# Start bytes of the standing weights: 108 and 364 instead of 224 and 512

## The chip, the cores and the metric

The kernel runs on one core of a Trainium2 chip. The metric is the device time of one launch in microseconds. Three runs of the kernel before gave 2774.83, 2776.44 and 2776.48 us, a median of 2776.44 us. Beside them stands one profiled execution of the same program, from which every row in this document is taken.

## The reference

The reference is a trunk of two decoder layers on 256 tokens of width 2048 in float32. Layer 0 mixes tokens by gated DeltaNet (16 key heads, 32 value heads of 128), layer 1 by HGRN2 (16 heads of 128); each mixer is followed by a SwiGLU feed-forward of width 5632. Cut to what matters here:

```python
h = x
for layer in range(2):
    n = rmsnorm(h, mixer_norm[layer])
    h = h + (gdn_mixer, hgrn2_mixer)[layer](n, ...)   # n @ w_in, recurrence in chunks, @ w_out
    h = h + swiglu(rmsnorm(h, ffn_norm[layer]), w_gate[layer], w_up[layer], w_down[layer])
return rmsnorm(h, final_norm)
```

Nearly all of the arithmetic is in the large products n @ w with weights that are read from HBM once. The products are wanted at close to float32 accuracy.

## The kernel before, in words

**How a large product is computed.** All weights come as halves of tiles, 128 partitions by 1024 float32 (512 KB). The function `stream` (line 587) walks through all halves of all groups in one list. For each half a DMA on SyncE's queue lands it in `raw`; ScalarE copies it to `wh`, rounded to the type float32r; VectorE writes what is left, raw - wh, to `wl`, again float32r. The activations are split in the same manner into `xt_h` and `xt_l` (in other stages `hth` and `htl`, `ot_h` and `ot_l`). A product is then three float32r products that add up in PSUM: high by high, high by low, low by high. There are four buffers each of raw, wh and wl, and loads run three halves ahead.

**Two ways to multiply.** `mm_rows` (line 624) lets the activations stand (128 by 128 tokens) and moves 512 weight columns per product; this covers the values and gates of the mixers, their output projections and the feed-forwards. `mm_cols` (line 652) lets 128 weight columns stand and moves all 256 tokens, so that the result comes out transposed, with features on the partitions. It serves the keys and queries of gated DeltaNet (8 groups) and the forget gates and queries of HGRN2 (8 groups). In one half it makes two 128-row blocks by four 128-column blocks by three products:

```python
for f in range(n_f):
    at = (k * n_f + f) * P
    for m, (w, s) in enumerate(((wh, xh), (wh, xl), (wl, xh))):
        self.nc.tensor.matmul(ps[...], w[:, at : at + P], s, ...)
```

Names in the profile read out<-moving,standing, so these products are main<-xt_h,wh, main<-xt_l,wh and main<-xt_h,wl. Each has a weight load of its own (PEld, LDWEIGHTS), also where two in a row use the same weights. Groups made with `cols=True` (lines 1292 and 1596) are the ones that use `mm_cols`. `mm_gates` (line 667) also lets weights stand, 64 columns wide, 48 products in all; its group is made without `cols=True`.

**Where wh and wl lie.** A partition of such a tile holds 1024 float32 (4096 bytes), and each tile is made 64 float32 (256 bytes, `PAD`) longer. The eight of them, alternately wh and wl, lie one behind the other and begin at byte 32 and byte 288 modulo 512 in turn. `make` (line 446) then chooses how many float32 to skip at the front so that the data begins at a wanted byte modulo 512, and `actual` (line 460) adds that skip to every access, of ScalarE, VectorE and TensorE alike:

```python
n = v.pool.padded.setdefault((v.tag, v.slot), len(v.pool.padded))
at = 32 + n * v.pad * 4 % 512
want = IN_COLS[v.tag] if v.cols else 32 + n % 2 * 512
v.skip = (want - at) // 4
```

For groups with `cols=True` the wanted bytes are those of `IN_COLS` (line 77); for all others both tiles begin at 32 modulo 512 (544 is 32 modulo 512). The same buffer can serve both kinds in turn, with another skip each time. A block of 128 columns is 512 bytes, so every block that stands begins at the same byte modulo 512 as its tile; in the gates a block is 256 bytes, so that blocks begin at 32 and 288 in turn. The token tiles xt_h and xt_l, whose slices are 1024 bytes, lie at byte 32 modulo 512 throughout, as follows from the sizes of the tiles allocated ahead of them; so do the tiles w and dec of the DeltaNet stage.

**What sets the order.** The whole program is recorded first; a planner (`plan`, line 308) then places every instruction on its engine by a list of costs (`price`, line 260) and due times, and the order that comes out is issued as written. The costs are computed from shapes and kinds of instruction. The large products form one fixed sequence on TensorE; the small products of the recurrences (aux in the profile) are put between them.

Of the kernel before, what the change touches and what calls it, by code (L numbers as in the profile page):

```python
# [73 lines left out]


PAD = 64
IN_COLS = {"wh": 224, "wl": 512}


class Op:  # L80
# [68 lines left out]
class Recorder:  # L149
# [296 lines left out]
    def make(self, v):  # L446
# [3 lines left out]
        if v.pad:  # L450
# [4 lines that stand above are left out]
# [1306 lines left out]
```

## Time and profile before

| what | value |
|---|---|
| median of three runs | 2776.44 us |
| span of the profiled execution | 2773.0 us |
| TensorE busy | 2757.2 us, 99% |
| weight loads under way | 2340.8 us, 84% |
| VectorE busy | 1901.0 us, 69% |
| ScalarE busy | 1428.3 us, 52% |
| products with 128 weight columns standing | 3 x 1024 |
| products with 512 weight columns moving, in main | 3 x 2176, 3 x 664 and 3 x 384 |

The profile's own record of the execution is the span, from the first to the last instruction; it stands 3.4 us under the median of the runs. All instructions carry line 490, where the recorded program is issued, so groups are told apart by the names of their tiles and by their shapes. A group's row gives busy time and the mean length of one record, then the idle time of the engine ahead of it and who ended it. Records of products overlap on TensorE, so a mean length isn't the pace; the pace is read from starts in the timeline or from a piece of the chain with its count. Products with standing weights fill TensorE from 8.9 us on in stretches up to 1898 us, between stretches with moving weights.

### The profile page before, as it was taken

The numbers are of one execution on the slowest core, as the hardware profiler recorded it, in microseconds if no ns is written. First come the engines' busy times: TensorE is split into PE (matmuls) and PEld (weight loads), VectorE is DVE, ScalarE is ACT, GpSimd is POOL, SyncE is SP. The second block draws the span as 40 slices with busy tenths as digits, with TensorE's granted clock in tenths as the row PEclk, the third lists the DMA queues.
The fourth block names the chain that finished last, engine by engine and source line by source line (L and its number), as shares of the span: only waits on it lengthen the run. The fifth ranks groups of instructions, "written<-read, shape, count | busy, mean of one in ns | idle before, by whom it ended". The sixth has DMA issues, their size and how long they took to land.

```text
span 2773.0 us, 41091 instructions
## 1 busy us (share of the span) xinstructions
PE 2757.2 (99%) x15662; PEld 2340.8 (84%) x15662; DVE 1901.0 (69%) x2857; ACT 1428.3 (52%) x2010; POOL 251.2 (9%) x370
## 2 busy tenths in 40 slices
PE   9999999999999999999999999999999999999998
PEld 9888888888888888888888989988888888888887
DVE  6787888878766666546665687778656675456764
ACT  6656666565554444344444556556454444344443
POOL 1213222232110000000000100000110000000000
PEclk9999999999999999999999999999999999999999
DMA  7686568786676555666556645545675556665564
GB/s 256 196 280 223 183 214 278 213 276 217 223 255 208 192 195 192 225 222 195 192 194 218 217 164 175 169 166 175 226 265 192 196 192 210 222 208 194 193 201 160
DMA packets 162677, 580.52 MB, mean 209 GB/s; under 512 B 20138, under 2 KB 21306, under 8 KB 162352
## 3 DMA queue, kind: packets, MB, share of 16 engines
q1 hardware_dynamic: 138912, 503.15, 55.4%
q0 software_dynamic: 23280, 73.91, 8.4%
q8 instruction: 122, 2.00, 0.3%
q10 hardware_dynamic: 288, 0.85, 0.1%
q14 instruction: 75, 0.61, 0.1%
HBM read 550.52 MB, written 27.31 MB: 208 GB/s over the span
## 4 chain that ended last, share of the span: by engine, by line
PE 99%; ACT 0%; DVE 0%; issue 0%; POOLq 0%; POOL 0%; ACTq 0%
PE main L490 92%; PE aux L490 6%; ACT dec L490 0%; DVE wl L490 0%; ACT wh L490 0%; ACT xt_h L490 0%; DVE utmp L490 0%; DVE u L490 0%; DVE pre L490 0%; ACT y L490 0%; POOLq L1757 0%; ACT junk L490 0%; DVE xl L490 0%; POOL coll L490 0%; DVE xt_l L490 0%
## 5 line engine op out<-in xcount | busy, mean ns | idle before, releaser
L490 DVE TENSOR_TENSOR wl<-raw,wh 128x1024 fp32r<-128x1024 f32 x945 | 1160.6, 1229 | 759.8 <-ACT wh L490 749.1
L490 ACT ACTIVATE wh<-raw 128x1024 fp32r<-128x1024 f32 x945 | 1000.7, 1060 | 1233.3 <-PE main L490 1137.5
L490 PE MATMUL main<-wh,xt_h 128*128 128x512 f32 x2176 | 849.3, 390 | 0.6 <-ACT wh L490 0.6
L490 PE MATMUL main<-wl,xt_h 128*128 128x512 f32 x2176 | 848.3, 390 | 1.5 <-DVE wl L490 1.5
L490 PE MATMUL main<-wh,xt_l 128*128 128x512 f32 x2176 | 849.5, 390 | 0.0
L490 PEld LDWEIGHTS main<-wl,xt_h 128*128 128x128 f32 x2176 | 408.4, 188 | 85.8 <-DVE wl L490 1.8
L490 PEld LDWEIGHTS main<-wh,xt_h 128*128 128x128 f32 x2176 | 408.5, 188 | 85.1 <-ACT wh L490 1.0
L490 PEld LDWEIGHTS main<-wh,xt_l 128*128 128x128 f32 x2176 | 408.5, 188 | 84.4
L490 PE MATMUL main<-xt_h,wl 128*128 128x256 f32 (+1 forms) x1040 | 292.2, 281 | 1.3 <-DVE wl L490 1.3
L490 PE MATMUL main<-xt_l,wh 128*128 128x256 f32 (+1 forms) x1040 | 291.8, 281 | 0.3 <-DVE xt_l L490 0.3
L490 PE MATMUL main<-xt_h,wh 128*128 128x256 f32 (+1 forms) x1040 | 290.5, 279 | 0.4 <-ACT wh L490 0.4
L490 PE MATMUL main<-wh,htl 128*128 128x512 f32 x664 | 258.6, 389 | 0.0
L490 PE MATMUL main<-wl,hth 128*128 128x512 f32 x664 | 258.3, 389 | 0.0
L490 PE MATMUL main<-wh,hth 128*128 128x512 f32 x664 | 258.3, 389 | 0.0
L490 PEld LDWEIGHTS main<-xt_h,wh 128*128 128x128 f32 (+1 forms) x1040 | 195.6, 188 | 0.9 <-ACT wh L490 0.6
L490 PEld LDWEIGHTS main<-xt_h,wl 128*128 128x128 f32 (+1 forms) x1040 | 193.7, 186 | 1.9 <-DVE wl L490 1.8
L490 PEld LDWEIGHTS main<-xt_l,wh 128*128 128x128 f32 (+1 forms) x1040 | 193.8, 186 | 1.0 <-DVE xt_l L490 0.5
L490 DVE STREAM_TRANSPOSE turned<-h 32x256 f32<-32x256 f32 x352 | 153.5, 436 | 7.2
L490 PE MATMUL main<-wh,ot_l 128*128 128x512 f32 x384 | 151.2, 394 | 0.0
L490 PE MATMUL main<-wh,ot_h 128*128 128x512 f32 x384 | 150.6, 392 | 0.0
L490 PE MATMUL main<-wl,ot_h 128*128 128x512 f32 x384 | 150.5, 392 | 0.0
L490 PEld LDWEIGHTS main<-wl,hth 128*128 128x128 f32 x664 | 124.6, 188 | 25.9
(206 smaller groups left out, 2250.6 us busy)
## 6 DMA issues: line engine op xcount, KB each, us to landing
raw<-in_ffn_gu SPq DMA_DIRECT2D x352, 512.0 KB, 3.7
raw<-in_ffn_d SPq DMA_DIRECT2D x176, 512.0 KB, 4.6
raw<-in_hgrn_in SPq DMA_DIRECT2D x128, 512.0 KB, 3.8
raw<-in_gdn_kq SPq DMA_DIRECT2D x64, 512.0 KB, 5.5
raw<-in_gdn_v SPq DMA_DIRECT2D x64, 512.0 KB, 4.7
raw<-in_gdn_z SPq DMA_DIRECT2D x64, 512.0 KB, 5.0
raw<-in_gdn_out SPq DMA_DIRECT2D x64, 512.0 KB, 5.0
x_home<-x POOLq DMA_DIRECT2D x36, 512.0 KB, 5.7
```

Source lines behind the costliest of these rows:

```text
L490: getattr(getattr(tc.nc, op.eng), op.method)(*args, **kw)
```

## The change

Two constants change. In groups with `cols=True`, wh begins at byte 108 modulo 512 instead of 224, and wl at byte 364 instead of 512 (that is, 0 modulo 512). The skips become 19 float32 for both, instead of 48 for wh and 56 for wl. All sizes, buffers and instructions stay as they are.

```diff
 PAD = 64
-IN_COLS = {"wh": 224, "wl": 512}
+IN_COLS = {"wh": 108, "wl": 364}
```

## The prediction

> **What bounds the kernel now.** I read the page's first part, the waits of TensorE, the chain that ended last, then the groups by shape, and last single stretches of the timeline.
>
> ```profile
> span 2773.0 us, 41091 instructions
> ...
> PE 2757.2 (99%) x15662; PEld 2340.8 (84%) x15662; DVE 1901.0 (69%) x2857; ACT 1428.3 (52%) x2010; POOL 251.2 (9%) x370
> ...
> PEclk9999999999999999999999999999999999999999
> ```
> ```profile
> PE main L490 <- DVE wl L490: 2.8, 3, 1.5
> PE aux L490 <- POOL ones L490: 1.1, 1, 1.1
> PE main L490 <- ACT wh L490: 1.0, 2, 0.6
> ```
>
> TensorE is busy 99% of the span, its granted clock in the top tenth throughout, and all that it ever waited for the split weights is 2.8 + 1.0 us. So nothing upstream (loads, splits) sets the time. The only way in which this change can move the end is the time that one product takes. The medians of the runs stand 3.4 us above this profiled span (2776.4 against 2773.0), so a change in the span is added to 2776.4.
>
> The change touches the products in which a tile of weights stands: names main<-xt_h,wh, main<-xt_l,wh and main<-xt_h,wl, 256 tokens wide.
>
> ```profile
> L490 PE MATMUL main<-xt_h,wl 128*128 128x256 f32 x1024 | 287.7, 281 | 0.9 <-DVE wl L490 0.9
> L490 PE MATMUL main<-xt_l,wh 128*128 128x256 f32 x1024 | 287.3, 281 | 0.0
> L490 PE MATMUL main<-xt_h,wh 128*128 128x256 f32 x1024 | 285.8, 279 | 0.4 <-ACT wh L490 0.4
> ...
> L490 PE MATMUL aux<-w,dec 128*128 128x128 f32 x192 | 22.7, 275 | 0.0
> ```
> ```profile
> L490 PEld LDWEIGHTS main<-xt_h,wh 128*128 128x128 f32 x1024 | 193.5, 189 | 0.9 <-ACT wh L490 0.6
> L490 PEld LDWEIGHTS main<-xt_l,wh 128*128 128x128 f32 x1024 | 191.6, 187 | 0.4
> L490 PEld LDWEIGHTS main<-xt_h,wl 128*128 128x128 f32 x1024 | 191.6, 187 | 1.2 <-DVE wl L490 1.1
> ...
> L490 PEld LDWEIGHTS main<-xt_h,wh 128*64 128x64 f32 x16 | 2.2, 134 | 0.0
> ```
>
> There are 3 x 1024 = 3072 of them, each with its own weight load. The means are lengths of one record, and records overlap, so the pace has to be read from starts. Two pieces of the chain in order of time give it (start, length, count): the first lies among products with standing weights, the second among those where 512 weights move and 128 tokens stand.
>
> ```profile
> 34.66 12.00 PE main L490 x102
> ```
> ```profile
> 549.27 21.55 PE main L490 x95
> ```
>
> 12.00 us / 102 = 117.65 ns for a product with standing weights; 21.55 / 95 = 226.8 ns for one with moving weights. So 3072 x 117.65 ns = 361 us of the span, 13%, is what the change can touch. One nanosecond on each product is 3.07 us, 0.11% of the kernel. In a stage of such products the loads are dense too:
>
> ```profile
> 549.30:570.80 21.50, 21.50 (x96) 17.79 (x96) 17.68 (x32) 19.27 (x44) 6.57 (x10) 1.00 0.83 272
> 1551.50:1598.00 46.50, 46.50 (x397) 46.49 (x396) 32.39 (x50) 29.94 (x36) 7.85 (x11) 1.00 0.64 208
> ```
>
> (Columns: stretch, its length, then PE, PEld, DVE, ACT and POOL busy with counts.) From 1551.5 us on a weight load is under way 46.49 of 46.50 us; among the moving weights 17.79 of 21.50. A load of 128 columns takes 187 to 189 ns and one of 64 takes 134: some 54 ns for 64 columns, 0.84 ns a column, about 108 ns for 128. A product with standing weights thus reads 128 x 512 B of weights and 128 x 1024 B of tokens in the same 117.65 ns, with hardly any slack on either side. This is where a start byte could matter.
>
> **The change part by part.** It removes and adds no instruction, byte or wait. The planner's costs depend on shapes alone, so the order of all instructions stays. What moves is where wh and wl lie inside their own padded tiles: skip 48 and 56 floats become 19 and 19. Both starts are multiples of 32 bytes before; after it both lie 12 bytes past one (108 = 3 x 32 + 12, 364 = 11 x 32 + 12). Four things touch these bytes.
>
> (1) ScalarE writes wh and VectorE writes wl, now from such a start. The trace has a VectorE write of the same size that starts 12 bytes into its tile, pre (line 949, columns 3 and on):
>
> ```profile
> L490 DVE TENSOR_TENSOR wl<-raw,wh 128x1024 fp32r<-128x1024 f32 x945 | 1160.6, 1229 | 759.8 <-ACT wh L490 749.1 <-PE aux L490 3.2
> ...
> L490 DVE TENSOR_TENSOR x<-x,main 128x1024 f32<-128x1024 f32 x39 | 47.6, 1220 | 19.5 <-PE main L490 19.3
> ...
> L490 DVE TENSOR_TENSOR pre<-main,rstd_row 128x1024 f32<-128x1024 f32 x8 | 9.8, 1220 | 3.6 <-PE main L490 3.6
> ```
>
> It takes 1220 ns, as the add into x from an even start does. I cost the writes and VectorE's read of wh at nothing. Cover, if I am wrong: VectorE is busy 32.39 of 46.50 us in the stage quoted, so each of its 50 instructions could grow by 280 ns before TensorE would wait.
>
> (2) DMAs write raw only, which does not move: nothing.
>
> (3) The moving-weight products and the gates (line 667, 64 columns wide) keep their positions: nothing.
>
> (4) TensorE's weight loads read from the new start while the tokens of the product before stream by. This is the whole sum. No row shows a load from such a start, so it is bounded. Lower end: the quickest products in the trace that load 128 columns of 4 bytes each time are those of w and dec; with them stand the gates, whose tokens stream as here but with 64 weight columns.
>
> ```profile
> 383.72 1.50 PE L490 MATMUL aux<-w,dec 128*128 128x128 f32 x12
> ```
> ```profile
> 9.95 0.28 PE L490 MATMUL main<-xt_h,wh 128*64 128x256 f32 x1
> ...
> 10.64 0.28 PE L490 MATMUL main<-xt_h,wh 128*64 128x256 f32 x1
> ```
>
> Twelve in 1.50 us, the last one 275 ns long, are (1.50 - 0.275) / 11 = 111.4 ns apart. If the new starts took away all disturbance above that pace, 117.65 - 111.4 = 6.25 ns go, x 3072 = -19.2 us. Upper end: the kernel's own price (line 269, 0.0133 us + n / 2400) says 226.6 ns for 512 columns, and the trace has 226.8; its split is 213.3 of streaming and 13.3 on top. For 256 columns it says 106.7 + 13.3 = 120.0. Products with standing weights run at 117.65, so 11.0 on top. The gates step 0.69 us in 6, 115 ns, so 8.3 on top for half the weight columns. The surplus goes with weight columns loaded under a stream: 13.3 per 128 in the moving products, 16.6 by the gates doubled, 11.0 with wh at 224 and wl at 0. The first two have every operand at byte 32 or 288 modulo 512; the third has the positions that the change gives up. Doubling the gates' surplus is the upper end: 106.7 + 16.6 = 123.3 ns, +5.65 x 3072 = +17.4 us.
>
> Between -19.2 and +17.4 I take the price that the other full-rate products pay, 120.0 ns: two families of rows pay at least that surplus, and only the positions given up pay less. +2.35 ns x 3072 = +7.2 us. All other edits come to nothing, so the sum is 2776.4 + 7.2 = 2783.6 us, a span of 2780.2.
>
> A rule that bears on this is in the Trainium skill, "SBUF — State Buffer", Specifications and the note on cachelines: 16-byte lines, of which each wants at least two hits, and a penalty for crossing to a new one. A load of 512 bytes from 108 touches 33 such lines instead of 32 and hits the first once. By that alone I estimate one more column time, 0.84 ns x 3072 = +2.6 us, against the +7.2 that I take from rows; nothing in this trace shows a line's size.
>
> **The rivals.**
>
> Fewer collisions (faster). A load that is 12 bytes off the tokens' boundaries may ask for its lines in cycles where the stream doesn't. For it: the surplus is not fixed; it already is 11.0 here and 13.3 elsewhere, with position the visible difference, and the load's length differs between 187 and 189 ns inside one triple of products. Against it: nothing shows a position that does better than the one given up. Any pace from 111.4 to 115.8 ns belongs to it: -19.2 to -5.7 us; midway 113.6 ns, -12.4 us, 2764.0. It decides as soon as a product loses 1.8 ns, 0.2% of the kernel (5.6 us), about what a measurement can tell from no change.
>
> Positions don't matter (no change). The surplus could be a fixed cost of loading 128 columns back to back, and the distance between 11.0 and 13.3 a matter of width, not of bytes. For it: 115 ns at starts 32 and 288 alike in the gates. Against it: gates with half of the columns should then pay half of 11.0, not 8.3. Time 2776.4. The Trainium skill, "TensorE: Matmul & The Clock Gate", Part 2, step 1, says the same: two independent read ports, so that a load takes nothing from the running matmul. The trace agrees only in part, with a surplus that follows the columns loaded.
>
> Every read straddles two lines (much slower). If weights are fetched in blocks, each block off its boundary might need two accesses, and the surplus of 11.0 doubles: +11.0 x 3072 = +33.8 us, 2810. For it: all of TensorE's operands stand on multiples of 32 bytes so far. Against it: pre's 1220 ns.
>
> **How the numbers follow.** Forecast 0.38, its own range 2782 to 2794 (119.5 to 123.3 ns a product). Straddling 0.07. No effect within 1.8 ns a product 0.21. Fewer collisions 0.34. So slower 0.38 + 0.07 = 0.45, same 0.21, faster 0.34. The range runs from 2760, below which I leave 0.08 of the fast case, to 2792, above which lie the straddling case and 0.03 of the forecast: 0.82 inside.
>
> **What would show it.** In the profile after: the piece that begins near 34.66 us with 102 products should last 12.2 us instead of 12.00 (11.6 if collisions go, 13.1 if reads straddle); the three x1024 groups, 279 to 281 ns now, should grow by up to 2 ns in mean length; the stage of 384 such products near 1551.5 should take 0.9 us more; the 226.8 ns of moving weights, the gates' 115 and VectorE's 1229 and ScalarE's splits must stay. If the whole difference isn't 3072 times the change in pace, or if waits for wh or wl appear, the account is wrong; a pace below 115.8 would refute the choice of 120.0.

## The result, and the profile after

The changed kernel took 2769.11 us (median of 12 runs, 2768.12 to 2770.07), the kernel before 2775.74 beside it (12 runs, 2774.44 to 2777.17): a ratio of 0.9976 with a 95% interval of 0.9968 to 0.9984. It is faster by 6.6 us, 0.24%, where the forecast was slower by 7.2. The profiled execution has a span of 2766.0 us against 2773.0.

First the page's head, the waits of TensorE for split weights, and the groups of the moved products, all of the changed kernel:

```profile
span 2766.0 us, 41091 instructions
...
PE 2749.6 (99%) x15662; PEld 2333.5 (84%) x15662; DVE 1899.9 (69%) x2857; ACT 1428.6 (52%) x2010; POOL 251.6 (9%) x370
```
```profile
PE main L490 <- DVE wl L490: 2.2, 2, 1.3
PE main L490 <- ACT wh L490: 1.5, 2, 0.8
```
```profile
L490 PE MATMUL main<-xt_h,wh 128*128 128x256 f32 x1024 | 285.9, 279 | 0.7 <-ACT wh L490 0.7
L490 PE MATMUL main<-xt_h,wl 128*128 128x256 f32 x1024 | 285.6, 279 | 0.9 <-DVE wl L490 0.9
L490 PE MATMUL main<-xt_l,wh 128*128 128x256 f32 x1024 | 285.4, 279 | 0.0
```

The waits are 3.7 us, as before 3.8, and TensorE's busy time fell by 7.6 us, while VectorE's fell by 1.1 and ScalarE's rose by 0.3. So the gain is TensorE's pace. Two pieces of the chain in order of time (start, length, count) give it, the first for standing weights, the second for moving weights:

```profile
33.98 11.22 PE main L490 x99
```
```profile
543.16 21.55 PE main L490 x95
```

11.22 / 99 = 113.3 ns instead of 117.65; the moving weights have 226.8 as they had. With 113.3 everywhere the kernel should have gained 4.35 ns x 3072 = 13.4 us. It got half of that, and two stretches of standing weights show why. The rows give start and end of a stretch, its length, and TensorE's busy time with the count of products; each count holds the two or three products that still run at the left edge. Before, then after:

```profile
1670.00:1690.00 20.00, 20.00 (x172) 1.00 0.54 179
1565.00:1585.00 20.00, 20.00 (x172) 1.00 0.63 209
```
```profile
1660.00:1680.00 20.00, 20.00 (x169) 1.00 0.54 176
1557.50:1577.50 20.00, 20.00 (x179) 1.00 0.66 216
```

In 20 us a pace of 113.3 ns makes 176.5 products, 117.7 makes 170 and 120.0 makes 167. Before, both stretches run at 117.7. After, one runs at 113.3 and the other, with the same shapes, bytes and clock, at 120.0. The timeline of the changed kernel (start, length, product) shows where one turns into the other:

```profile
1858.37 0.28 PE L490 MATMUL main<-xt_h,wl 128*128 128x256 f32 x1
1858.48 0.28 PE L490 MATMUL main<-xt_h,wh 128*128 128x256 f32 x1
1858.60 0.28 PE L490 MATMUL main<-xt_l,wh 128*128 128x256 f32 x1
1858.71 0.28 PE L490 MATMUL main<-xt_h,wl 128*128 128x256 f32 x1
1858.83 1.04 PE L490 MATMUL aux<-head,zs 128*128 128x128 f32 x8
1859.62 0.36 PE L490 MATMUL main<-xt_h,wh 128*128 128x256 f32 x1
1859.82 0.28 PE L490 MATMUL main<-xt_l,wh 128*128 128x256 f32 x1
1859.94 0.28 PE L490 MATMUL main<-xt_h,wl 128*128 128x256 f32 x1
1860.06 0.28 PE L490 MATMUL main<-xt_h,wh 128*128 128x256 f32 x1
1860.18 0.28 PE L490 MATMUL main<-xt_l,wh 128*128 128x256 f32 x1
```

Up to 1858.83 the starts are 0.11 to 0.12 apart, 113.3 ns on the mean. Then come eight transposes of zs (head_out, the heads' outputs), and behind them every start is 0.12 us after the last, for all 261 products of that stretch. Three stretches of 261 products stand behind transposes of zs (from 1659.4, 1759.5 and 1859.6 us), one of 60 behind transposes of x (from 1549.3); these four run at 120.0 ns, nearly all others at 113.3 after a few products of 117 to 122. By starts of neighbours over about 3000 pairs in all, the mean pace went from 117.70 to 115.36 ns: 2.34 ns x 3072 = 7.2 us, and the spans differ by 7.0. Start times tell the same as a running account: the changed kernel leads by 5.3 us at the stretch of 99 products at 470 us, by 7.8 at 1659, loses 0.6 in each of the three stretches of 261, wins some 0.5 back between them, and ends 7.0 ahead.

### The profile page after: what moved, and what is told of

Same layout as the page of the kernel before. It is cut to its first block, busy times and chain, and to the rows that moved or that the text cites. A ratio compares the mean times of both kernels' runs of the same rounds, so it can differ in the third digit from the quotient of the medians.

```text
span 2766.0 us, 41091 instructions
## 1 busy us (share of the span) xinstructions
PE 2749.6 (99%) x15662; PEld 2333.5 (84%) x15662; DVE 1899.9 (69%) x2857; ACT 1428.6 (52%) x2010; POOL 251.6 (9%) x370
## 4 chain that ended last, share of the span: by engine, by line
PE 99%; ACT 0%; DVE 0%; issue 0%; DMA 0%; SPq 0%; POOLq 0%; POOL 0%; ACTq 0%
PE main L490 92%; PE aux L490 6%; ACT dec L490 0%; DMA first<-in_x 0%; DVE wl L490 0%; ACT wh L490 0%; DVE utmp L490 0%; SPq L490 0%; DVE pre L490 0%; ACT xt_h L490 0%; DVE u L490 0%; ACT y L490 0%; POOLq L1757 0%; ACT junk L490 0%; DVE xl L490 0%
## 5 line engine op out<-in xcount | busy, mean ns | idle before, releaser
L490 DVE TENSOR_TENSOR wl<-raw,wh 128x1024 fp32r<-128x1024 f32 x945 | 1160.7, 1229 | 755.6 <-ACT wh L490 742.2
L490 ACT ACTIVATE wh<-raw 128x1024 fp32r<-128x1024 f32 x945 | 1000.8, 1060 | 1226.9 <-PE main L490 1126.3
L490 PEld LDWEIGHTS main<-wh,hth 128*128 128x128 f32 x664 | 124.7, 188 | 25.9
```

What stands on the lines that cost most here:

```text
L490: getattr(getattr(tc.nc, op.eng), op.method)(*args, **kw)
```

## The experiments

All kernels are the kernel before with other start bytes, except where the text names the changed kernel as the base. Instructions, bytes and their order on every engine stay the same, unless a diff says otherwise. "Pace" is the mean distance between starts of neighbouring products with standing weights.

**Where the weights begin.** Three kernels separate the 12 bytes from the place: aligned places near the new ones (first line added), the old places plus 12 (second), and 32 and 288, the bytes that the forecast's price came from (third).

```diff
-IN_COLS = {"wh": 224, "wl": 512}
+IN_COLS = {"wh": 96, "wl": 352}
+IN_COLS = {"wh": 236, "wl": 524}
+IN_COLS = {"wh": 32, "wl": 288}
```

> wh begins at 96 and wl at 352 modulo 512: nearly the places of the change, but on multiples of 32 bytes. Theory A (what counts is that the starts lie 12 bytes past a multiple of 32): no product runs at the 113 ns of the changed kernel; all lie between 117 and 120 ns, 2774 to 2783 us. Theory B (what counts is the coarse place, wh and wl at the same place modulo 256): as the changed kernel, 113 ns in most stretches and 120 ns behind the transposes of zs, 2769 us.

> wh begins at 236 and wl at 524: the places of the kernel before, each moved on by 12 bytes. Theory A: paces of 113 and 120 ns as in the changed kernel, about 2769 us. Theory B: the paces of the kernel before, a steady 117.7 ns over three products, 2776 us.

> wh begins at 32 and wl at 288, as in the products that move weights and in the gates. The step of my prediction that took 120.0 ns for any place but 224 and 512 expects 120 ns in all 3072 products, 2783 us. Theory A expects something between 117 and 120 ns, 2776 to 2783 us, with no stretch at 113 ns. Theory B says nothing of it.

| starts | median us | ratio, 95% interval | mean pace, ns |
|---|---|---|---|
| 96 / 352 | 2772.14 | 0.9987, 0.9978 to 0.9996 | 116.1 |
| 236 / 524 | 2783.16 | 1.0024, 1.0015 to 1.0034 | 119.9 |
| 32 / 288 | 2782.69 | 1.0024, 1.0015 to 1.0034 | 119.9 |

Standing 12 bytes past a boundary is neither needed for the gain nor enough for it. The aligned kernel has the pace of 113.3 too, but in other stretches it runs at 117.8; the old places plus 12 lose. Both expectations for the latter, 2769 and 2776 us, were missed. With 32 and 288 the products run at 120.0 ns throughout: the price that the prediction took is the true price of that place. Stretches of 20 us of the aligned kernel (behind zs, then the stretch from 1560 us), then of the even one (behind zs):

```profile
1664.00:1684.00 20.00, 20.00 (x172) 1.00 0.53 172
1561.00:1581.00 20.00, 20.00 (x179) 1.00 0.65 213
```
```profile
1672.00:1692.00 20.00, 20.00 (x169) 1.00 0.52 176
```

**A scan over places.** Each of the 16 groups with standing weights got a place of its own, wl 256 bytes behind wh in nearly all of them.

```diff
-            want = IN_COLS[v.tag] if v.cols else 32 + n % 2 * 512
+            want = v.cols[v.tag == "wl"] if v.cols else 32 + n % 2 * 512
...
+        for g, pair in zip([g for g in groups if g.cols], SCAN, strict=True):
+            g.cols = pair
```

> Each of the 16 groups of standing weights has a place of its own, the same skip for wh and wl: 0, 4, 8, 1, 2, 3, 16, 32 float32 in the eight groups of the first layer, 5, 6, 7, 11, 12, 24, 27, 35 in those of the second. Theory A: the groups whose skip is no multiple of 8 (of 4, if the block is 16 bytes) show stretches at 113 ns, the others none. Theory B: the paces go by the coarse place, alike for 0 to 7, and groups at 11 to 27, around the 19 of the change, are the fast ones.

> Places around the change, group by group: skips 18, 20, 22, 21, 14 for both tiles in the first five groups of the first layer, then the pairs 108 and 352, 96 and 364, 224 and 480; in the second layer two groups each with skips 13, 18, 20 and 17. If the 113 ns state belongs to a range of places, skips 17, 18 and 20 show it in the first layer as 16 and 19 do; a place at which also the stretches behind the transposes of zs run at 113 ns would beat the change by up to 5 us. If it belongs to single places, most of these groups run at 116 to 120 ns.

One execution each, 2777.66 and 2776.74 us. Neither theory of the first scan holds: its only group at 113.3 ns begins at 96, a multiple of 32, while 76 and 80, near the change, run at 117.8. Steady pace by the byte at which wh begins (two numbers: different stretches of one group, or groups in both layers; 96 and 108 also from the kernels of their own):

| wh at | 32 | 36 | 40 | 44 | 48 | 52 | 56 | 60 | 64 |
|---|---|---|---|---|---|---|---|---|---|
| ns | 120.0 | 118.3 | 115.6 | 116.7 | 118.3, 120.0 | 120.0 | 121.9 | 116.7 | 118.3 |

| wh at | 76 | 80 | 84 | 88 | 96 | 100 | 104 | 108 | 112 |
|---|---|---|---|---|---|---|---|---|---|
| ns | 117.8 | 117.8 | 113.3, 120.0 | 117.8 | 113.3, 117.8 | 118.3 | 118.3 | 113.3, 120.0 | 118.8, 120.0 |

| wh at | 116 | 120 | 128 | 140 | 160 | 172 | 224 (wl 480) |
|---|---|---|---|---|---|---|---|
| ns | 120.0 | 116.7 | 117.3 | 120.0, 122.2 | 118.7, 120.0 | 116.7 | 117.8 |

In both scans the stretch from 1578 us is one group in steady pace, with wh at 56 in the first and at 84 in the second (166 products to 179 in 20 us):

```profile
1578.00:1598.00 20.00, 20.00 (x166) 1.00 0.57 182
```
```profile
1578.00:1598.00 20.00, 20.00 (x179) 1.00 0.61 198
```

113.3 ns is the lowest steady pace of these products in any kernel here. It belongs to single places, 84, 96 and 108, with 88, 100 and 104 between them at 117.8 to 118.3; 92 and 72 weren't tried as starts of wh. A step of 4 bytes off such a place costs 4.5 to 6.7 ns. Since a place can have two paces and most places were read in few stretches of one execution, a faster pace of a place that looks slow here isn't ruled out. Two pairs with another distance between wh and wl, 108/352 and 96/364, had two or three paces each, 113.3 and 120.0, and 113.3 and 117.2 to 117.8.

**wh and wl apart.** If each product paid by the place of its own weights, moving wh alone (first line) would give two thirds of the gain, and moving wl alone (second line) a third.

```diff
+IN_COLS = {"wh": 108, "wl": 512}
+IN_COLS = {"wh": 224, "wl": 364}
```

> Only wh moves (108), wl stays at 512. Theory P (each weight load pays by its own place): two of three products get the gain, from 117.7 to about 114.8 ns in the mean over three, 2767.5 to 2772 us. Theory J (the train of three loads settles into a state together): no such share; a state of its own, anywhere from 113 to 122 ns.

> Only wl moves (364), wh stays at 224. Theory P: one of three products gets the gain, from 117.7 to about 116.3 ns in the mean over three, 2771 to 2774 us. Theory J: a state of its own, anywhere from 113 to 122 ns.

With wh alone moved: 2773.42 us, 0.9992 (0.9983 to 1.0002), 117.0 ns in every stretch. With wl alone: 2773.87 us, 0.9993 (0.9984 to 1.0003), and three steady paces, 113.3, 117.8 and 120.0 by stretch. Here the stretch behind zs and the one from 1562.8 us with wl alone moved:

```profile
1666.00:1686.00 20.00, 20.00 (x169) 1.00 0.54 174
1564.00:1584.00 20.00, 20.00 (x179) 1.00 0.67 220
```

The median with wl alone lies inside what a price by each product's own place would give (2771 to 2774 us); it is the stretches that speak against such a price, and so does the run with wh alone, whose 117.0 ns stand against 114.8. A product's price isn't its own: with wl moved alone, the products of wh, two of three, run at 113.3 too, from the old place 224. The three products of a block settle on a pace jointly.

**What sets which pace.** Base is the changed kernel. The last of eight transposes ahead of a stretch (for the last head of the second pair) is made as a plain product with the identity, which has the same result. The cost that the planner sees is kept at the transpose's, so the order of all instructions is the same.

```diff
...
+                    if b and h and tt:
+                        nc.tensor.matmul(to, of, self.ident, start=True, stop=True)
+                    else:
+                        nc.tensor.transpose(to, of, self.ident)
```

> The changed kernel (108 and 364), where one of the eight transposes of zs in each batch is made as a plain product with the identity, the planner's price and the order unchanged. In two of the three long stretches of the second layer that run at 120 ns (261 products each, behind transposes of zs) the plain product is now the last one ahead of them; in the third a transpose is still the last. Theory S (the products have two steady states, and how a stretch is entered decides which): the first two run at 113.3 ns, 2 x 261 x 6.67 ns = 3.5 us less, the third and the short one behind the transposes of x stay at 120 ns; with some 12 x 0.12 us for the plain products about 2767 us. Theory G (something else in these groups makes them slow): all stay at 120 ns, about 2770.5 us.

2765.60 us (4 runs), 0.9962 of the kernel before (0.9947 to 0.9977). All three stretches of 261 products turned from 120.0 to 113.3 ns, although nothing in them was touched; the one of 60 behind x, where the transposes stayed, kept 120.0. A miss: the third stretch was to stay as well, since in its batch the plain product is fifth of eight with transposes behind it. It turned like the others, so it is not the last product that decides. Twelve batches got a plain product where three needed one. To use it only where a stretch is slow (zs in HGRN), and to try it on one batch of x too:

```diff
+                    if scale == 0.5 and b and h and tt:
...
+                    if norm == 2 and cg == 3 and pair and k and tt:
```

> The changed kernel with a plain product instead of the last transpose of a batch in five batches only: the four of zs in HGRN (three of them ahead of a stretch of 261 products at 120.0 ns) and that of x ahead of the 60 products at 1549.3 us. The order of all instructions stays. If a plain product among the transposes sets the pace of the stretch behind it, whatever tile is transposed: all four stretches run at 113.3 ns, also the one behind x, which no run has turned yet; 843 x 6.7 ns = 5.6 us go, five plain products cost 0.1 us each more, so the median is about 5.1 us under that of the changed kernel, 2764.0 us (2763 to 2765). If something of zs alone did it: the stretch behind x stays at 120.0 ns (0.4 us more). If the earlier run's gain came from its twelve plain products and not from the pace: no better than 2765.6.

2763.74 us (5 runs), 0.9957 of the kernel before (0.9943 to 0.9970): the lowest median of the study, 5.4 us under the changed kernel. The lead over the version with twelve plain products, whose runs overlap with these, is not clear of noise. All four stretches now run at 113.3 ns, the one behind x included. Timeline, and a stretch of 20 us in the first batch of 261, of this kernel:

```profile
1857.75 0.28 PE L490 MATMUL main<-xt_h,wl 128*128 128x256 f32 x1
1857.87 1.15 PE L490 MATMUL aux<-head,zs 128*128 128x128 f32 x9
1858.78 0.36 PE L490 MATMUL main<-xt_h,wh 128*128 128x256 f32 x1
1858.98 0.28 PE L490 MATMUL main<-xt_l,wh 128*128 128x256 f32 x1
1859.09 0.28 PE L490 MATMUL main<-xt_h,wl 128*128 128x256 f32 x1
1859.20 0.28 PE L490 MATMUL main<-xt_h,wh 128*128 128x256 f32 x1
1859.32 0.28 PE L490 MATMUL main<-xt_l,wh 128*128 128x256 f32 x1
```
```profile
1662.00:1682.00 20.00, 20.00 (x178) 1.00 0.54 183
```

The plain product shows as one record more (x9 instead of x8) and takes 0.11 us more; behind it the starts are 0.11 to 0.12 apart instead of 0.12. The profiled executions of these two kernels (spans 2764.6 and 2763.5) gained less on the changed kernel's 2766.0 than their pace says, since in both some 2.6 to 3.3 us more passed up to the end of the first layer, where the chain now has short pieces of VectorE and of a load of raw; the medians agree with the pace.

**Do the moving weights pay by place too?** Base is the changed kernel; each group with 512 moving weights got a pair of starts (ROWS), nearly all of them different; the line for want is that of the scan.

```diff
...
+        rows = iter(ROWS)
+        for g in groups[1:]:
+            g.cols = IN_COLS if g.cols else next(rows)
```

> The changed kernel, in which every group that moves its weights also gets a place of its own for wh and wl: the same skip for both, 0 to 64 float32, in the first 65 such groups, then random pairs. The standing groups keep 108 and 364. Theory W (the surplus of these products depends on places too): some groups run at a pace well off the 226.7 ns of today, such as 220 ns, one step of 6.67 ns lower, which over 9792 products would be worth up to 65 us. Theory F (with one load in twice the time the surplus of 13.3 ns is fixed): all groups stay at 226 to 227 ns.

One execution, 2829.62 us. They do. Three stretches of moving products, with starts at 228/484, 224/480 and 32/288, then the long piece of the chain that holds most of the feed-forward, first of this kernel, then of the changed kernel:

```profile
1262.00:1282.00 20.00, 20.00 (x85) 1.00 0.59 186
1240.00:1260.00 20.00, 20.00 (x88) 1.00 0.73 240
112.50:132.50 20.00, 20.00 (x90) 1.00 0.66 196
```
```profile
840.53 656.13 PE main L491 x2808
```
```profile
827.96 636.50 PE main L490 x2808
```

By starts the three stretches run at 240.0, 233.4 and 227.0 ns; the long pieces at 233.7 and 226.7 a product. None is below the 226.7 that these products have today, so a hope for a gain there falls. What looked like a fixed price of streaming plus 13.3 ns is the price of the old place, and no place tried has a lower one.

**Place of the weights, or distance to the tokens?** The token tiles move by 64 bytes, to 96 modulo 512, and the standing weights with them, to 172 and 428. In the scan, 172/428 with tokens at 32 had 116.7 ns; the distance is that of the change, 76 bytes.

```diff
-IN_COLS = {"wh": 224, "wl": 512}
+IN_COLS = {"wh": 172, "wl": 428}
...
+        nc.gpsimd.memset(t([P, 16], "space0"), 0.0)
...
+        nc.gpsimd.memset(t([P, 112], "space1"), 0.0)
```

> All token tiles xt_h and xt_l begin 64 bytes later (96 instead of 32 modulo 512), and wh and wl of the standing groups too (172 and 428), so that the distance between tokens and weights is that of the changed kernel. Theory R (the distance between the two counts): the stretches of the changed kernel, 113.3 ns and behind the transposes of zs 120 ns, a span near 2767 us. Theory N (the place of the weights by itself counts): the 116.7 ns that the scan showed for 172 and 428 against tokens at 32, a span near 2770 us.

One execution, 2808.79 us. Standing weights first (behind zs), then a piece of the chain among moving weights, whose tokens now stand at 96 while the weights are still at 32:

```profile
1689.00:1709.00 20.00, 20.00 (x178) 1.00 0.56 182
```
```profile
899.86 100.33 PE main L490 x430
```

Standing weights run at 113.3 ns, behind zs and x also; of the larger stretches none is slow (one of 34 products, from 229.6 us, is at 120.0). So in the one pair of kernels that tells the two apart, the pace that can be reached goes with the distance between the two operands, 76 bytes in both, and not with the place of the weights. Which of two paces a stretch falls into didn't go with the distance: behind zs the change has 120.0, this kernel 113.3. The moving products pay for the same move: 100.33 / 430 = 233.3 ns instead of 226.7, which is what makes this kernel slow as a whole. Both expected spans, near 2767 and 2770 us, were missed for that reason.

## Why the prediction was wrong

**The step that failed** is step (4), at its choice between the bounds: "I take the price that the other full-rate products pay, 120.0 ns". The price is right for the place it came from; 32/288 measured 119.9 over all stretches and 2782.69 us, within a microsecond of the forecast's 2783.6. But both families of rows behind it had their operands at a distance of 0 or 256 bytes, and that they paid more than the third was read as "only the positions given up pay less". The scan has 113.3 to 122 ns, by single places 4 bytes apart. From one family at one better place nothing followed for a third place. The choice was refuted by the mark set beforehand, a pace below 115.8: the mean is 115.36, the piece near 34 us 113.3.

**The second family was misread.** The gates' 115 ns came from six steps right behind a wait, which include the slower steps with which a stretch begins. Later in the same stage of the kernel before, from start to start over 21 steps:

```profile
14.13 0.28 PE L490 MATMUL main<-xt_h,wh 128*64 128x256 f32 x1
...
16.51 0.28 PE L490 MATMUL main<-xt_h,wh 128*64 128x256 f32 x1
```

2.38 us / 21 = 113.3 ns, so the settled surplus is 6.7 and not 8.3; doubled it is 13.3, and the upper end would have been the 120.0 itself instead of 123.3. The pace of 113.3 thus stood in the trace of before, for products with 64 standing columns. Nor were w and dec the quickest products with a load of 128 columns: the transposes of x and zs step some 109 ns in the same trace.

**A second assumption, unspoken:** that a place has one pace. After the change there are two, and the mean lies between by the share of products in the slower stretches. This is why the gain is 6.6 us and not the 13.4 that the piece near 34 us alone would say, nor the 12.4 of the rival's midway case.

**What held.** No wait appeared and the groups with moving weights kept 226.8; the difference is 3072 times the change of mean pace (7.2 us against 7.0 of span). Writes from 12 bytes past a boundary cost nothing measurable; the page of the changed kernel has, as before, 1229 ns for VectorE's remainder and 1060 for ScalarE's copy, and although only 128 of the 945 halves moved, either total differs by no more than 0.1 us:

```profile
L490 DVE TENSOR_TENSOR wl<-raw,wh 128x1024 fp32r<-128x1024 f32 x945 | 1160.7, 1229 | 755.6 <-ACT wh L490 742.2
L490 ACT ACTIVATE wh<-raw 128x1024 fp32r<-128x1024 f32 x945 | 1000.8, 1060 | 1226.9 <-PE main L490 1126.3
```

The lower bound of 111.4 ns was low by 1.9 only, and the rival of fewer collisions named the direction and the place of the gain, at the upper edge of its paces; its reason, the 12 bytes, is not borne out, since 96/352 reaches 113.3 and 236/524 doesn't. One marker was of no use: the mean lengths of the x1024 groups went from 279 and 281 to 279, since a record is longer than the pace and hides it.

**The rivals.** That positions don't matter falls with every run above: the order of work is the same, and the paces reach from 113.3 to 122.2 ns. Its companion, the rule of two independent read ports in the Trainium skill, "TensorE: Matmul & The Clock Gate", Part 2, step 1, is not borne out here: with loads and streams otherwise unchanged, the distance of their start bytes moves a standing product between 113.3 and 122 ns and a moving one between 226.7 and 240. That every read straddles two lines falls with 113.3 ns at 108. The 16-byte lines of the Trainium skill, "SBUF — State Buffer", Specifications and the note on cachelines, don't order the places either: wh at 32, 48, 64, 80 and 112, all on multiples of 16, run at 117.8 to 120.0, and of such places only 96 reaches 113.3, while 84 and 108, which are not on multiples of 16, reach it too.

**What stays open** is the mechanism. Shown are that the places of the two operands relative to each other count, that three products settle jointly, and that one plain product in place of a transpose ahead of a stretch switches it between two steady paces. Whether its kind does this or its extra record and 0.11 us, which move the moment at which the stretch begins, no run separates. The slow pace doesn't belong to transposes as such: with the tokens moved along, the same eight transposes of zs have 113.3 ns behind them, and the 34 products at 120.0 ns stand behind plain products (r, u):

```profile
228.82 1.05 PE L490 MATMUL aux<-r,u 128*128 128x128 f32 x8
229.63 0.36 PE L490 MATMUL main<-xt_h,wh 128*128 128x256 f32 x1
229.83 0.28 PE L490 MATMUL main<-xt_l,wh 128*128 128x256 f32 x1
229.95 0.28 PE L490 MATMUL main<-xt_h,wl 128*128 128x256 f32 x1
```

Which of load and stream waits for the other, and why 113.3 comes at 84, 96 and 108 and not at the places tried between, no view of the profile shows either.

## What to carry to other kernels

Where a matmul and the weight load of the next one read at the same time, a start byte can be worth 4 to 8% of a product at no instruction's cost, as it was here; it is found by a scan that gives each group its own place, and not by reasoning from alignment. Scan in the real stream and read the pace in every stretch, by what runs ahead of it, since one place can have two steady paces. Where a long stretch has the slower one, try another kind for one small product ahead of it: here that gave about 5.4 us for five products. And read a pace where it has settled, not from the first steps behind a wait.

## What the runs showed of the hardware

A train of equal products on TensorE has a memory: with operands, clock and order unchanged, 261 products ran at 120.0 or at 113.3 ns to their end, depending on whether the eight small products ahead held one plain product, with its one record and 0.11 us more, or were all transposes. With the kernel's old places the train always fell into the same pace, 117.7 ns on the mean, which is why the trace of before gave no sign of a second one. And the products with 512 moving weights, whose 226.8 ns had looked like a floor set by width, lost up to 13 ns each with other places of their weights.
